# A fifth weight buffer, another place for the first pair of chunks, and later block sums in a one-layer encoder kernel

## The chip, the cores and the metric

The kernel runs on one core of one Trainium2 chip. A core has a matrix engine (TensorE, PE in the rows; PEld are its weight loads), a vector engine (VectorE, DVE), a scalar engine (ScalarE, ACT), GpSimd (POOL) and a sync engine (SyncE, SP), which here only issues DMA transfers. Each engine works through its own queue in order; semaphores tie the queues together. The metric is the device time of one execution in microseconds (us), lower is better.

## The reference

One layer of an encoder on 256 tokens of width 1024, all in float32:

```
x <- x + 1/2 * RMSNorm(SwiGLU(RMSNorm(x)))      first FFN, w_in 1024 x 5632, w_down 2816 x 1024
x <- x + RMSNorm(mix(RMSNorm(x)))               gated recurrence and forgetting attention, merged
x <- x + RMSNorm(CrossAttn(RMSNorm(x), mem))    memory of 256 rows, 4 heads
x <- x + 1/2 * RMSNorm(SwiGLU(RMSNorm(x)))      second FFN

def swiglu(h, w_in, w_down):
    gate, up = jnp.split(h @ w_in, 2, axis=-1)
    return (jax.nn.silu(gate) * up) @ w_down
```

## The kernel before

Every float32 product is made of three matmuls. An operand is split into a rounded part `hi` and the rest `lo`; the product is hi·hi + hi·lo + lo·hi. ScalarE makes `hi` by a cast, VectorE makes `lo` by a subtraction (`load_split`, lines 128 to 138, and `split`, lines 154 to 156). So each weight tile of 128x1024 (512 KB) goes DMA into a `raw` buffer, ScalarE cast, VectorE subtraction, TensorE. There are four `raw` buffers, eight `hi` and eight `lo` buffers, and two `wide` buffers of twice a raw's size. Activations and sums lie in 21 tiles of the pool `data` (`m4`).

The FFN (`ffn`, lines 384 to 695) has 11 chunks of 256 hidden columns. A plain chunk (`act_tok`) takes four weight tiles and 48 matmuls of 512 columns; the down-projection of a chunk (`down`, two further tiles, two token halves) takes 24. Two chunks in a row can be made together as a pair (`quad`, lines 425 to 581) by a Winograd-like scheme: 7 products of 12 matmuls in place of 8, at the price of sums of weight blocks and of activations (`mixed`, lines 288 to 316). `QUADS_1` names the chunks at which pairs begin in the first FFN, here 3, 6 and 9; the second FFN reads sums that were made earlier and stored in DRAM.

In the first FFN the weight sums are made within the pair. For each of two halves q, two tiles come into `raw` (the blocks B11 and B21) and two into one `wide` buffer. VectorE adds: t1 = B11 + first wide block (line 485), t2 = t1 + second wide block (line 465), t4 = t2 - in place with B21 (line 467), and for the third product the two wide blocks (line 498). `rest` makes t2 and t4 together: for q = 0 at once, for q = 1 behind the first down-projection in the code. TensorE then runs: B11 and B21 (24 matmuls, into `b1` and `b3`), the t1 product (12), half of a down-projection (12), the t2 product (12), its other half (12), the product of the wide sums, a whole down-projection (24), the product with the lower wide blocks (`lower`), and the t4 product. `keep` copies a PSUM bank on ScalarE; line 545 adds `b3` to the first of these copies, `p1`. The raw buffers of a pair stay in use until t4 is made, the wide buffers until `lower` is split.

At the head (lines 700 to 725) eight tiles `head` bring x transposed and the first weights. Four of them lie in the four raw buffers, four in the two wide buffers. ScalarE and VectorE split them; then eight ScalarE copies with a gain make `full1`, the unsplit activations that `mixed` reads.

Instructions are put in order by a scheduler that goes by priorities, buffers and dependences; `tc.issue_after(i)` keeps an instruction behind instruction i. So an edit in the code can move instructions at other places too. On SP's queue loads stand in one order, and a load whose buffer is not free holds up those behind it.

Of the kernel before, what the change touches and what calls it, by code (L numbers as in the profile page):

```python
# [9 lines left out]
F32 = mybir.dt.float32  # L10
# [3 lines left out]
ALU = mybir.AluOpType  # L14
AX = mybir.AxisListType

P = 128
D = 1024
T = 256
KB = D // P  # L20
# [28 lines left out]
X_AT = 11  # L49


QUADS_1 = (3, 6, 9)
QUADS_2 = (3, 5, 7, 9)

SUMS_AT = (
# [22 lines left out]
def block_kernel(ctx: ExitStack, tc: tile.TileContext, wts, head_in, gf_in, x_in, mem_in, memT_in, cols, rows, fbias, masks, out):  # L78
    nc = tc.nc
    V, S, G, PE = nc.vector, nc.scalar, nc.gpsimd, nc.tensor  # L80

    cp = ctx.enter_context(tc.tile_pool(name="consts", bufs=1))
    wp = ctx.enter_context(tc.tile_pool(name="weights", bufs=4))
    mp = ctx.enter_context(tc.tile_pool(name="data", bufs=21))
    sp = ctx.enter_context(tc.tile_pool(name="small", bufs=8))
    dp = ctx.enter_context(tc.tile_pool(name="dram", bufs=1, space=bass.MemoryType.DRAM))
    pp = ctx.enter_context(tc.tile_pool(name="psum", bufs=2, space=bass.MemoryType.PSUM))
# [14 lines left out]
    def nm(s):  # L102
        count[0] += 1
        return f"{s}_{count[0]}"
# [22 lines left out]

    def load_split(src, n=512):

        raw = wp.tile([P, D], F32, tag="raw", name=nm("raw"), bufs=4)  # L130
        hi, lo = parts_of()
        r, h, l = raw, hi, lo
        if n < 512:
            r, h, l = (p.rearrange("p (k n) -> p k n", k=2)[:, :, :n] for p in (raw, hi, lo))
        loads.append(nc.sync.dma_start(r, src).ins)
        S.copy(h, r)  # L136
        V.tensor_tensor(out=l, in0=r, in1=h.bitcast(F32), op=ALU.subtract)  # L137
        return hi, lo
# [245 lines left out]
    def ffn(w_in, w_dn, X, full, r2, n_tok, i_row, quads, sums, first_half, second_half=None):  # L384
# [40 lines left out]
        def quad(c, n_down):  # L425
# [12 lines left out]
            if sums:  # L438
                for i in range(4):
                    hi, lo = load_split(wts[_AT[w_in] + 4 * c + i - 4])  # L440
                    B11.append((hi[:, :512], lo[:, :512]))
                    B21.append((hi[:, 512:], lo[:, 512:]))

                def sum_of(k):
                    W = wp.tile([P, 2, D], F32, tag="wide", name=nm("wide"), bufs=2)
                    for q in range(2):
                        with tc.issue_after(loads[-1]):
                            loads.append(nc.sync.dma_start(W[:, q], sums[c][(0, 3, 2, 1)[k], q]).ins)
                    return two(W[:, 0].rearrange("p (i n) -> p i n", i=2)) + two(W[:, 1].rearrange("p (i n) -> p i n", i=2))

                def lower():
                    out = []
                    for q in range(2):
                        u = _AT[w_in] + 4 * c + 2 * q
                        raw = wp.tile([P, D], F32, tag="raw", name=nm("raw"), bufs=4).rearrange("p (i n) -> p i n", i=2)
                        loads.append(nc.sync.dma_start(raw, wts[u : u + 2, :, 512:].rearrange("i p n -> p i n")).ins)
                        out += two(raw)
                    return out

                summed = None  # L460
            else:
                wide, made = [], [[], [], []]

                def rest(W, raws, t1, t2, t4):
                    V.tensor_tensor(out=t2, in0=t1, in1=W[:, :, 1], op=ALU.add)  # L465
                    for i in range(2):
                        V.tensor_tensor(out=t4[:, i], in0=t2[:, i], in1=raws[i][:, 512:], op=ALU.add)  # L467

                for q in range(2):
                    W = wp.tile([P, 2, 2, 512], F32, tag="wide", name=nm("wide"), bufs=2)  # L470
                    raws = []
                    for i in range(2):
                        u = _AT[w_in] + 4 * c + 2 * q + i
                        raw = wp.tile([P, D], F32, tag="raw", name=nm("raw"), bufs=4)
                        loads.append(nc.sync.dma_start(raw, wts[u - 4]).ins)
                        loads.append(nc.sync.dma_start(W[:, i].rearrange("p j n -> p (j n)"), wts[u]).ins)
                        hi, lo = parts_of()
                        split(hi, lo, raw)
                        B11.append((hi[:, :512], lo[:, :512]))
                        B21.append((hi[:, 512:], lo[:, 512:]))  # L480
                        raws.append(raw)
                    wide.append(W)
                    t1, t2, t4 = (m4([P, 2, 512], n="sum") for _ in range(3))
                    for i in range(2):
                        summed = V.tensor_tensor(out=t1[:, i], in0=raws[i][:, :512], in1=W[:, i, 0], op=ALU.add).ins  # L485
                    for k, t in zip((0, 1, 2), (t1, t2, t4)):
# [43 lines left out]
            b1, b2, b3 = mm(), mm(), trp()  # L530
            n = len(log)
# [10 lines left out]
                    flush(n + L_ACT)  # L542
            p1 = keep(b1)
            prods(b2, F(s1h, s1l), T1, True)
            V.tensor_tensor(out=p1, in0=p1, in1=b3, op=ALU.add)
# [15 lines left out]
            n = len(log)  # L561
# [16 lines left out]
            n = len(log)  # L578
# [50 lines left out]
        for c in range(n_tok, NFF):  # L629
# [9 lines left out]
            if c == 2 and first_half:  # L639
                n = len(log)  # L640
# [4 lines left out]
            else:  # L645
                for h in range(2):
                    n = len(log)
# [16 lines left out]
            while done < min(c - 1, NFF - STAG):  # L664
                n = len(log)
# [32 lines left out]


    X1 = Pair()  # L700
    heads = [wp.tile([P, D], F32, tag="raw", name=nm("head"), bufs=4) for kb in range(4)]
    for _ in range(2):
        wide = wp.tile([P, 2, D], F32, tag="wide", name=nm("head"), bufs=2)
        heads += [wide[:, 0], wide[:, 1]]
# [15 lines left out]
        gain_split(X1, kb, heads[kb][:, :T], heads[kb][:, T + 512 + kb : T + 512 + kb + 1], first=kb == 0)  # L720
        lo_last = V.tensor_tensor(out=lo, in0=w, in1=hi.bitcast(F32), op=ALU.subtract).ins
    full1 = [m4([P, 4, T], n="full") for _ in range(2)]
    for kb in range(KB):
        with tc.issue_after(lo_last):
            S.activation(full1[kb // 4][:, kb % 4], heads[kb][:, :T], AF.Copy, scale=heads[kb][:, T + 512 + kb : T + 512 + kb + 1])

# [525 lines left out]
    for h in range(2):  # L1252
# [4 lines left out]
        for i in range(4):  # L1257
            for j in range(2):
                kb = 2 * i + j
# [59 lines left out]
    def second(m):  # L1319
        half(X4, r4, 1, G_F2, m + L_F2)  # L1320
# [87 lines left out]
```

## Time and profile before

| what | us |
| --- | --- |
| runs | 787.92, 788.52, 791.23 (median 788.52) |
| the profiled execution | 787.54 |
| its span in the trace | 785.8 |
| of that, TensorE busy | 772.8 |
| mean granted TensorE clock | 0.999 |
| first FFN, first matmul on real data to the last of its pairs | about 5 to 170 |
| last FFN | about 600 to 786 |

In rows of groups and of the timeline stand the start or the busy time, the engine, the line of the kernel, the operation, and its tiles as output<-inputs; in brackets stands how long the engine was idle before and which instruction ended that. A matmul's shown duration includes the pipeline's drain, so two in a row overlap; the rate is read from start to start. In stretches of time ("a:b") the columns are the length, the busy time and count of each engine, the granted clock, the DMA engines' share and GB/s.

### The profile page before, as it was taken

Reading aid. Unit: us, or ns where it says so; the run is one execution under the profiler, and the core shown is the slowest. Engines: PE = TensorE matmul, PEld = TensorE weight load, DVE = VectorE, ACT = ScalarE, POOL = GpSimd, SP = SyncE. Lnnn points to the kernel's source line nnn. Section 1 sums busy time; section 2 is a strip of 40 time slices with the busy share of each in tenths; the row PEclk is TensorE's granted clock in tenths of the full one; section 3 lists DMA queues with packets and bytes.
Section 4 is the critical chain, followed back from the end, with each engine's and each line's share of the span. In section 5 each row is a group of like instructions: output and inputs, shape, how many; then the busy total and the mean of one; then the engine's idle time right before and its main releaser. Section 6 shows DMA issues by size and latency. Waiting matters only on the chain.

```text
span 785.8 us, 13132 instructions
## 1 busy us (share of the span) xinstructions
PE 772.8 (98%) x4984; PEld 665.8 (85%) x4984; DVE 647.1 (82%) x998; ACT 475.3 (60%) x715; POOL 48.1 (6%) x80
## 2 busy tenths in 40 slices
PE   9999999999999899999999999999999999999996
PEld 7868888877899899998888888999888888888885
DVE  6899898999788788578678887997797988888864
ACT  7757566576654356446685434754655767777752
POOL 0000000000111100200001221012110000000000
PEclk9999999999999999999999999999999999999999
DMA  7848649348688554673389999579966199889931
GB/s 268 299 186 261 225 156 305 119 152 302 252 305 299 184 176 143 216 261 108 133 281 331 375 365 363 200 260 360 361 201 210 57 335 366 323 276 325 348 113 55
DMA packets 57391, 193.61 MB, mean 246 GB/s; under 512 B 6248, under 2 KB 9712, under 8 KB 57328
## 3 DMA queue, kind: packets, MB, share of 16 engines
q1 hardware_dynamic: 48080, 159.60, 58.1%
q0 software_dynamic: 9104, 33.04, 11.8%
q8 instruction: 39, 0.64, 0.3%
q14 instruction: 24, 0.20, 0.1%
q10 hardware_dynamic: 144, 0.13, 0.1%
HBM read 174.92 MB, written 17.83 MB: 245 GB/s over the span
## 4 chain that ended last, share of the span: by engine, by line
PE 87%; DVE 5%; DMA 3%; ACT 2%; issue 1%; SPq 0%; DVEq 0%; ACTq 0%
PE mm L92 59%; PE acc L92 22%; PE tr L92 3%; DMA raw<-in_wts_dram 2%; DVE lo L156 2%; PE tr L324 1%; PE tr L399 1%; DMA head<-in_head_dram 1%; DVE lo L137 1%; ACT hi L136 1%; DVE sum L467 0%; DVE at L420 0%; DVE sum L465 0%; DVE sum L485 0%; DVE act L156 0%
## 5 line engine op out<-in xcount | busy, mean ns | idle before, releaser
L137 DVE TENSOR_TENSOR lo<-raw,hi 128x1024 fp32r<-128x1024 f32 (+1 forms) x220 | 261.1, 1201 | 57.6 <-ACT hi L136 53.9
L136 ACT CAST hi<-raw 128x1024 fp32r<-128x1024 f32 (+1 forms) x220 | 223.9, 1035 | 126.0 <-PE mm L92 65.7
L92 PE MATMUL mm<-hi,lT 128*128 128x512 f32 (+1 forms) x424 | 161.0, 384 | 2.1 <-issue 2.1
L92 PE MATMUL mm<-lo,hT 128*128 128x512 f32 (+1 forms) x424 | 161.9, 385 | 1.1 <-DVE lo L156 1.1
L92 PE MATMUL mm<-hi,hT 128*128 128x512 f32 (+1 forms) x424 | 161.4, 384 | 0.0
L92 PE MATMUL acc<-hi,act 128*128 128x512 f32 x352 | 113.3, 391 | 0.2 <-ACT hi L136 0.2
L92 PE MATMUL mm<-hT,lo 128*128 128x256 f32 x384 | 109.0, 284 | 0.0
L92 PE MATMUL mm<-hT,hi 128*128 128x256 f32 x384 | 109.0, 284 | 0.0
L92 PE MATMUL mm<-lT,hi 128*128 128x256 f32 x384 | 108.9, 284 | 0.0
L92 PEld LDWEIGHTS mm<-hi,hT 128*128 128x128 f32 x424 | 79.6, 188 | 17.4 <-issue 2.3
L92 PEld LDWEIGHTS mm<-lo,hT 128*128 128x128 f32 x424 | 79.5, 188 | 15.5 <-DVE lo L156 1.5
L92 PEld LDWEIGHTS mm<-hi,lT 128*128 128x128 f32 x424 | 79.5, 188 | 14.9 <-DVE lT L286 0.5
L92 PEld LDWEIGHTS acc<-hi,act 128*128 128x128 f32 x352 | 65.8, 188 | 14.4 <-ACT hi L136 0.6
L92 PEld LDWEIGHTS mm<-hT,lo 128*128 128x128 f32 x384 | 73.6, 192 | 0.1
L92 PEld LDWEIGHTS mm<-lT,hi 128*128 128x128 f32 x384 | 73.6, 192 | 0.1
L92 PEld LDWEIGHTS mm<-hT,hi 128*128 128x128 f32 x384 | 73.6, 192 | 0.1
L92 PE MATMUL acc<-lo,act 128*128 128x512 f32 x176 | 69.0, 393 | 0.1
L156 DVE TENSOR_TENSOR lo<-wide,hi 128x1024 fp32r<-128x1024 f32 x44 | 52.3, 1217 | 4.2 <-ACT hi L155 3.8
L155 ACT CAST hi<-wide 128x1024 fp32r<-128x1024 f32 x44 | 45.8, 1052 | 12.6 <-PE mm L92 4.9
L790 POOL DMA_DIRECT2D sums<-wide x32 | 23.6, 737 | 362.8 <-DVE wide L787 245.1
L92 PE MATMUL mm<-lo,sh 128*128 128x512 f32 x112 | 44.0, 392 | 0.2 <-DVE lo L156 0.2
L92 PE MATMUL mm<-hi,sh 128*128 128x512 f32 x112 | 44.0, 393 | 0.0
(248 smaller groups left out, 1160.6 us busy)
## 6 DMA issues: line engine op xcount, KB each, us to landing
raw<-in_wts_dram SPq DMA_DIRECT2D x228, 512.0 KB, 5.2
sums<-wide POOLq DMA_DIRECT2D x32, 512.0 KB, 6.2
wide<-sums SPq DMA_DIRECT2D x32, 512.0 KB, 7.0
wide<-in_wts_dram POOLq DMA_DIRECT2D x28, 512.0 KB, 6.2
wide<-in_wts_dram SPq DMA_DIRECT2D x16, 512.0 KB, 6.8
raw<-in_gf_dram SPq DMA_DIRECT2D x12, 344.0 KB, 5.2
head<-in_head_dram SPq DMA_DIRECT2D x8, 388.0 KB, 6.1
grow<-in_rows_dram SPq DMA_DIRECT2D x4, 512.0 KB, 7.9
```

The costliest lines, as they stand in the source:

```text
L92: log.append(PE.matmul(*args, **kw).ins)
L136: S.copy(h, r)
L137: V.tensor_tensor(out=l, in0=r, in1=h.bitcast(F32), op=ALU.subtract)
L155: S.copy(hi, src)
L156: V.tensor_tensor(out=lo, in0=src, in1=hi.bitcast(F32), op=ALU.subtract)
L324: PE.transpose(ps[:, j * P : (j + 1) * P], src(kb), ident)
L399: PE.transpose(trv[:, j, h * P : (h + 1) * P], ats[c, h][:, j * P : (j + 1) * P], ident)
L790: G.dma_start(sums[u][2 * e : 2 * e + 2, q, :, i * 512 : i * 512 + 512].rearrange("k p n -> p k n"), W[:, e])
```

## The change

There is a fifth raw buffer, and the data pool has 20 tiles in place of 21. The first FFN's pairs begin at chunks 4, 6 and 9, so that chunk 3 is a plain chunk and the pairs at 4 and 6 stand back to back; before, chunk 5 lay between. `rest` is cut into `second` (t2) and `fourth` (t4). For q = 0 both still run at once. For q = 1 `second` stands where `rest` stood, and `fourth` goes to the place where the third product's sums are made; both these and it are kept behind the addition of line 545 by `issue_after(first[0])`, and the two sums of wide blocks now stand ahead of the splits of both. In the head, `full1[0]` is made by one VectorE addition of the split parts; ScalarE keeps its copies for the other four blocks only.

```diff
-QUADS_1 = (3, 6, 9)
+QUADS_1 = (4, 6, 9)
...
-    mp = ctx.enter_context(tc.tile_pool(name="data", bufs=21))
+    mp = ctx.enter_context(tc.tile_pool(name="data", bufs=20))
...
-        raw = wp.tile([P, D], F32, tag="raw", name=nm("raw"), bufs=4)
+        raw = wp.tile([P, D], F32, tag="raw", name=nm("raw"), bufs=5)
...
-                def rest(W, raws, t1, t2, t4):
+                def second():
                     V.tensor_tensor(out=t2, in0=t1, in1=W[:, :, 1], op=ALU.add)
+
+                def fourth():
                     for i in range(2):
                         V.tensor_tensor(out=t4[:, i], in0=t2[:, i], in1=raws[i][:, 512:], op=ALU.add)
...
                     if q == 0:
-                        rest(W, raws, t1, t2, t4)
+                        second()
+                        fourth()
...
-                    out = []
-                    for W in wide:
-                        V.tensor_tensor(out=W[:, :, 0], in0=W[:, :, 0], in1=W[:, :, 1], op=ALU.add)
-                        out += two(W[:, :, 0])
-                    return out
+                    with tc.issue_after(first[0]):
+                        for W in wide:
+                            V.tensor_tensor(out=W[:, :, 0], in0=W[:, :, 0], in1=W[:, :, 1], op=ALU.add)
+                        fourth()
+                    return two(wide[0][:, :, 0]) + two(wide[1][:, :, 0])
...
             T1 = sum_of(0)
+            first = []
...
-            V.tensor_tensor(out=p1, in0=p1, in1=b3, op=ALU.add)
+            first.append(V.tensor_tensor(out=p1, in0=p1, in1=b3, op=ALU.add).ins)
...
             if not sums:
-                rest(W, raws, t1, t2, t4)
+                second()
...
     full1 = [m4([P, 4, T], n="full") for _ in range(2)]
-    for kb in range(KB):
+    V.tensor_tensor(out=full1[0], in0=X1.h[0].bitcast(F32), in1=X1.l[0].bitcast(F32), op=ALU.add)
+    for kb in range(4, KB):
         with tc.issue_after(lo_last):
             S.activation(full1[kb // 4][:, kb % 4], heads[kb][:, :T], AF.Copy, scale=heads[kb][:, T + 512 + kb : T + 512 + kb + 1])
```

Where this moves instructions: first VectorE, in the pair at 6, from the second sums to the splits of the third product's sums. `sum` are t1, t2, t4; `wide` the wide buffers; `keep` is p1. The pair before:

```order
L156 TENSOR_TENSOR lo_1036<-sum_920,hi_1035 128x1024
L156 TENSOR_TENSOR act_766<-tr_982,act_766 128x512
L545 TENSOR_TENSOR keep_989<-keep_989,tr_957 128x512
L465 TENSOR_TENSOR sum_943<-sum_942,wide_927 128x1024
L420 SCALAR_TENSOR_TENSOR at_1006<-keep_989,r_301,sg_1004 128x256
L467 TENSOR_TENSOR sum_944<-sum_943,raw_928 128x512
L467 TENSOR_TENSOR sum_944<-sum_943,raw_935 128x512
L156 TENSOR_TENSOR lo_1040<-sum_943,hi_1039 128x1024
L156 TENSOR_TENSOR lo_1071<-wide_904,hi_1070 128x1024
L498 TENSOR_TENSOR wide_927<-wide_927 128x2x512
L156 TENSOR_TENSOR lo_1076<-wide_927,hi_1075 128x1024
```

The pair at the same place now:

```order
L548 TENSOR_TENSOR keep_983<-keep_983,tr_944 128x512
L137 TENSOR_TENSOR lo_1016<-raw_1014,hi_1015 128x1024
L420 SCALAR_TENSOR_TENSOR at_1000<-keep_983,r_298,sg_998 128x256
L465 TENSOR_TENSOR sum_930<-sum_929,wide_914 128x1024
L156 TENSOR_TENSOR lo_1028<-sum_907,hi_1027 128x1024
L500 TENSOR_TENSOR wide_891<-wide_891 128x2x512
L156 TENSOR_TENSOR lo_1032<-sum_930,hi_1031 128x1024
L500 TENSOR_TENSOR wide_914<-wide_914 128x2x512
L469 TENSOR_TENSOR sum_931<-sum_930,raw_915 128x512
L469 TENSOR_TENSOR sum_931<-sum_930,raw_922 128x512
L156 TENSOR_TENSOR lo_1066<-wide_891,hi_1065 128x1024
L156 TENSOR_TENSOR lo_1070<-wide_914,hi_1069 128x1024
```

The t4 additions (line 467, now 469) for q = 1 have gone behind the split of the second t2, and both sums of wide blocks (line 498, now 500) stand behind the p1 addition; before, the first of them stood between the t1 splits.

Next TensorE, in the same pair, at the t2 product and the down-projection half behind it. `mm` is the product's bank, `acc` the down-projection's, `sh` and `sl` the mixed activations, `act` the activations of an earlier chunk. Before, the twelve matmuls of the product stood together, and the down-projection half followed:

```order
L92 MATMUL mm_955<-hi_1035,sh_341 128x512
L92 MATMUL mm_955<-lo_1036,sh_341 128x512
L92 MATMUL mm_955<-hi_1035,sl_342 128x512
L92 MATMUL mm_955<-hi_1035,sh_341 128x512
L92 MATMUL mm_955<-lo_1036,sh_341 128x512
L92 MATMUL mm_955<-hi_1035,sl_342 128x512
L92 MATMUL mm_955<-hi_1039,sh_341 128x512
L92 MATMUL mm_955<-lo_1040,sh_341 128x512
```

Now:

```order
L92 MATMUL mm_942<-hi_1027,sh_434 128x512
L92 MATMUL acc_444<-hi_1003,act_608 128x512
L92 MATMUL acc_444<-lo_1004,act_608 128x512
L92 MATMUL acc_444<-hi_1003,act_608 128x512
L92 MATMUL acc_445<-hi_1003,act_608 128x512
L92 MATMUL mm_942<-lo_1028,sh_434 128x512
L92 MATMUL mm_942<-hi_1027,sl_435 128x512
L92 MATMUL mm_942<-hi_1027,sh_434 128x512
L92 MATMUL mm_942<-lo_1028,sh_434 128x512
L92 MATMUL mm_942<-hi_1027,sl_435 128x512
L92 MATMUL mm_942<-hi_1031,sh_434 128x512
L92 MATMUL acc_445<-lo_1004,act_608 128x512
```

Four matmuls of the down-projection stand ahead of the first `lo` of the second sums, and four more ahead of the second; the other four follow the product.

Last SP's queue, at the loads of the pair at 6. The loads of lines 475 and 476 (now 477 and 478) are the pair's raw and wide tiles, those of line 135 other weights. Before:

```order
L476 DMA wide_904<-in_wts_dram 128x1024 x2
L476 DMA wide_927<-in_wts_dram 128x1024
L135 DMA raw_866<-in_wts_dram 128x1024
L135 DMA raw_878<-in_wts_dram 128x1024
L475 DMA raw_905<-in_wts_dram 128x1024
L475 DMA raw_912<-in_wts_dram 128x1024
L475 DMA raw_928<-in_wts_dram 128x1024
L475 DMA raw_935<-in_wts_dram 128x1024
L476 DMA wide_927<-in_wts_dram 128x1024
```

Now:

```order
L477 DMA raw_892<-in_wts_dram 128x1024
L477 DMA raw_899<-in_wts_dram 128x1024
L477 DMA raw_915<-in_wts_dram 128x1024
L477 DMA raw_922<-in_wts_dram 128x1024
L135 DMA raw_1002<-in_wts_dram 128x1024
L478 DMA wide_891<-in_wts_dram 128x1024 x2
L478 DMA wide_914<-in_wts_dram 128x1024 x2
L135 DMA raw_1014<-in_wts_dram 128x1024
```

Three of the four wide loads stood ahead of the pair's raw loads; now all four stand behind them and behind a down-projection tile.

More of the change, by code (lines that the diff above doesn't have):

```diff
@@ L454, in lower @@
                         u = _AT[w_in] + 4 * c + 2 * q
-                        raw = wp.tile([P, D], F32, tag="raw", name=nm("raw"), bufs=4).rearrange("p (i n) -> p i n", i=2)
+                        raw = wp.tile([P, D], F32, tag="raw", name=nm("raw"), bufs=5).rearrange("p (i n) -> p i n", i=2)
                         loads.append(nc.sync.dma_start(raw, wts[u : u + 2, :, 512:].rearrange("i p n -> p i n")).ins)
@@ L473, in quad @@
                         u = _AT[w_in] + 4 * c + 2 * q + i
-                        raw = wp.tile([P, D], F32, tag="raw", name=nm("raw"), bufs=4)
+                        raw = wp.tile([P, D], F32, tag="raw", name=nm("raw"), bufs=5)
                         loads.append(nc.sync.dma_start(raw, wts[u - 4]).ins)
@@ L700, in block_kernel @@
     X1 = Pair()
-    heads = [wp.tile([P, D], F32, tag="raw", name=nm("head"), bufs=4) for kb in range(4)]
+    heads = [wp.tile([P, D], F32, tag="raw", name=nm("head"), bufs=5) for kb in range(4)]
     for _ in range(2):
```

## The prediction, made before the changed kernel was run

> **What bounds the kernel now.** I read the page's table of busy time first, then busy time by stretch, then where TensorE's own queue has holes, then what ends each hole.
>
> ```profile
> PE 772.8 (98%) x4984; PEld 665.8 (85%) x4984; DVE 647.1 (82%) x998; ACT 475.3 (60%) x715; POOL 48.1 (6%) x80
> ...
> 46.20:58.50 12.30, 10.67 (x46) 7.41 (x44) 12.30 (x16) 7.09 (x9) 0.00 (x0) 1.00 0.25 89
> 91.40:123.00 31.60, 31.60 (x142) 25.91 (x141) 30.15 (x34) 20.14 (x25) 0.00 (x0) 1.00 0.50 161
> 139.50:173.00 33.50, 33.18 (x149) 26.84 (x149) 32.10 (x37) 22.06 (x28) 0.00 (x0) 1.00 0.39 129
> 268.00:275.00 7.00, 4.92 (x153) 4.79 (x152) 4.62 (x8) 1.11 (x2) 2.27 (x6) 1.00 0.81 301
> 215.00:630.00 415.00, 412.80 (x3360) 372.56 (x3358) 334.96 (x582) 230.01 (x374) 44.76 (x70) 1.00 0.71 248
> 630.00:786.00 156.00, 148.72 (x676) 122.29 (x674) 122.03 (x144) 102.85 (x131) 0.00 (x0) 0.99 0.74 267
> ```
>
> The columns of a stretch are its length, then busy us of TensorE, weight loads, VectorE, ScalarE, GpSimd, then granted clock, DMA share, GB/s. TensorE is the bound, and the change removes no matmul. So only holes can be won. From 215 us on there are 2.2 us of them up to 630 and 7.3 after, most of those behind the last matmul. What is left lies in the first FFN, in two places:
>
> ```profile
> 16.09 0.61 PE L92 MATMUL acc<-lo,hT 128*128 128x512 f32 x2
> 17.27 0.73 PE L92 MATMUL acc<-hi,hT 128*128 128x512 f32 x2 [0.56 <-ACT hi L136]
> 18.59 0.73 PE L92 MATMUL acc<-lo,hT 128*128 128x512 f32 x2
> ...
> 28.68 0.61 PE L92 MATMUL mm<-hi,hT 128*128 128x512 f32 x2
> 29.13 0.62 PE L92 MATMUL mm<-hi,lT 128*128 128x512 f32 x2
> ...
> 50.05 0.39 PE L92 MATMUL mm<-hi,hT 128*128 128x512 f32 x1
> 51.55 0.50 PE L92 MATMUL mm<-lo,hT 128*128 128x512 f32 x1 [1.11 <-DVE lo L156]
> 55.75 1.22 PE L92 MATMUL acc<-hi,act 128*128 128x512 f32 x4 [0.22 <-ACT hi L136]
> 58.49 0.50 PE L92 MATMUL acc<-lo,act 128*128 128x512 f32 x1
> ...
> 102.04 0.60 PE L399 MATMUL tr<-ident,at 128*128 128x128 f32 x4
> 102.40 0.48 PE L92 MATMUL tr<-lo,hT 128*128 128x512 f32 x1
> ```
>
> Two matmuls take 0.45 from start to start (28.68 to 29.13), so one is 0.2265; four transposes take 0.36 (102.04 to 102.40). From 16.09 to 18.59 six matmuls should take 1.36 and took 2.50: **1.1 lost** at the head. From 50.05 to 58.49 the timeline has 23 matmuls and four transposes, 5.6 at that rate, and took 8.4: **2.9 lost** in the first pair (chunks 3 and 4). The chain of waits shows why:
>
> ```profile
> 33.76 7.07 DMA raw<-in_wts_dram
> 57.30 1.15 DVE lo L137
> 58.49 4.17 PE acc L92 x17
> ```
>
> Up to 58 us the path runs through weight loads and VectorE, afterwards through TensorE. In the stretch from 46.2 to 58.5 the loads run at 89 GB/s: all four raw buffers are held for the pair's sums, and the down-projection weights that TensorE takes at 55.75 and 58.49 come late. So 4.0 us is about all that this change can gain there, 0.5% of the time. A measurement of this kernel tells some 0.5%, 3.9 us, from no change.
>
> **The change part by part.** The fifth raw buffer and the head's copies:
>
> ```profile
> 0.75 4.26 SPq L706 DMA_DIRECT2D head<-in_head_dram  x8
> 11.66 3.44 SPq L135 DMA_DIRECT2D raw<-in_wts_dram  x4
> GB/s 0 91 279 392 334 381 381 403 414 144 8 153 342 295 218 299 371 397 422 404 386 408 379 273 269 76 73 259 197 240 361 288 262 335 397 430 415 415 422 397
> ...
> 13.78 2.50 ACT L725 ACTIVATE full<-head 128x256 f32<-128x256 f32 x6
> 16.18 1.03 ACT L136 CAST hi<-raw 128x1024 fp32r<-128x1024 f32 x1
> ```
>
> The GB/s row covers 0 to 45 us, 1.125 us a cell. The head tiles hold all four raw buffers, so the first weights are issued at 11.66, and the DMA engines nearly stop from 10 to 13.5 us. A fifth buffer lets one load follow the heads at 5 us; the others come free with the head splits instead of with ScalarE's copies. ScalarE makes its first weight cast at 16.18, right behind six copies; the change drops four copies of 0.41 (2.50 over six), 1.6 us, so that cast is ready near 15.6, before TensorE wants it at 16.5. VectorE gets one 128x1024 addition (1.14, below) between the head's splits, where it has idle time and TensorE is some 1 us behind it; that covers nearly all of it. Without cover it costs 1.1 and the head gains nothing. I take 1.1 won and 0.2 paid: **-0.9** (bounds -1.1 and 0).
>
> Pairs at 4, 6, 9. I follow VectorE's lead: from the end of the first split of a pair's weights to the first matmul that reads it.
>
> ```profile
> 32.52 1.21 DVE L137 TENSOR_TENSOR lo<-raw,hi 128x1024 fp32r<-128x1024 f32 x1
> 86.04 2.48 DVE L156 TENSOR_TENSOR lo<-raw,hi 128x1024 fp32r<-128x1024 f32 x2 [0.90 <-ACT hi L155]
> 104.90 0.67 DVE L545 TENSOR_TENSOR keep<-keep,tr 128x512 f32<-128x512 f32 x1
> 106.63 0.48 DVE L420 SCALAR_TENSOR_TENSOR at<-keep,r,sg 128x256 f32<-128x256 f32 x1
> 107.03 1.28 DVE L467 TENSOR_TENSOR sum<-sum,raw 128x512 f32<-128x512 f32 x2
> 108.23 1.21 DVE L156 TENSOR_TENSOR lo<-sum,hi 128x1024 fp32r<-128x1024 f32 x1
> 109.37 1.21 DVE L156 TENSOR_TENSOR lo<-wide,hi 128x1024 fp32r<-128x1024 f32 x1
> 112.95 1.23 DVE L156 TENSOR_TENSOR lo<-wide,hi 128x1024 fp32r<-128x1024 f32 x1 [1.24 <-ACT hi L155]
> 122.20 4.62 DVE L137 TENSOR_TENSOR lo<-raw,hi 128x1024 fp32r<-128x1024 f32 x4
> ...
> 97.28 0.39 PE L92 MATMUL mm<-lo,hT 128*128 128x512 f32 x1
> 110.00 0.39 PE L92 MATMUL mm<-lo,sh 128*128 128x512 f32 x1
> 127.88 0.40 PE L92 MATMUL mm<-lo,hT 128*128 128x512 f32 x1
> ```
>
> From start to start an operation on 128x1024 takes 1.14 (108.23 to 109.37), on 128x512 0.60 (half of 107.03 to 108.23), on 128x256 0.40 (106.63 to 107.03). In the pair at 6 the first split ends near 87.3 and is read at 97.28: a lead of 10.0. The second half of the second sums ends at 109.4 and is read at 110.0: 0.6. At the pair's end the next chunk's first split ends near 123.4, read at 127.88: 4.5. So a pair eats VectorE's lead and a plain chunk restores it; the first pair began with too little.
>
> The pair at 4: VectorE's order after the fourth split of chunk 2 (ends 33.7) has, up to the pair's first split: 11 of 1.14, 8 mix additions of about 0.37, 3 of 0.60, 2 of 0.40: 18.1, so 51.8. TensorE, from chunk 2's start at 28.68, has 144 matmuls and 12 transposes, 33.7, less 1.1 won at the head: 61.3. Lead 9.5, near the 10.0 seen. The largest fall inside a pair in the new order comes at the third sums: 14 of 1.14, 12 of 0.60, 3 of 0.40, 24.3 on VectorE, against 72 matmuls and 8 transposes, 17.0, on TensorE: 7.3. The 9.5 cover it. The 2.9 go: **-2.8**, with 0.1 left.
>
> The pair at 6, now directly behind it: From the one pair's first split to the other's VectorE has 33.2 (22 of 1.14, 11 of 0.60, 4 of 0.40), TensorE 30.6 (132 matmuls, 8 transposes): the lead falls to 6.9. By the row at 122.20 it would be 4.5. The fall of 7.3 then leaves TensorE waiting 0.4 or 2.8. TensorE's new order helps at the second sums (down-projection matmuls now stand between their halves), which is why the bottleneck moves to the third. I take **+1.2**, nearer the sum, because the idle 1.24 of the row at 112.95 was the wait for a cast right behind a sum of wide blocks, and that sum now stands earlier.
>
> The third and fourth products' sums behind the first product's addition: the same additions, later: the third sums' two of 1.14 and the fourth's two of 0.60. In the pair at 6 of before, 2.3 us of them stood ahead of what TensorE read next. In the pair at 9 nothing in front of it has moved, and its holes of 0.3 in 33.5 (above) can shrink: **-0.2** (0 to -0.3). They now wait for that addition, which waits for the pair's first 24 matmuls and ScalarE's copy; behind it on VectorE stand a down-projection split and the second sums, for which TensorE waits. By the sums above VectorE gets there 6.9 us of TensorE time into the first pair, just when it is ready, and 1 us after that in the second: a few tenths at most. Raw buffers are held longer for it; the fifth pays for that.
>
> One data tile less: TensorE's order from the mix stage to the second FFN is unchanged; the second FFN has loads issued earlier and no hole to fill: 0, bounds +-0.5.
>
> Sum: -0.9 -2.8 +1.2 -0.2 = **-2.7**. The profiled execution took 787.54 (span 785.8, 1.7 around it), so 784.8 by its own time. The median of the runs shown, 788.52, lies 1.0 higher; between the two I put **785.5**.
>
> **The rivals.**
> (1) The second pair gives it back: its hole is 2.8 and more, because the lead at its start is the 4.5 of the row rather than 6.9. For it: that row was measured. Against: that pair's VectorE also idled 1.24. Net -1 to +0.5: 788.
> (2) All holes close: the lead of 9.5 is there and the second pair loses nothing: -4.1, 784.0.
> (3) Slower: the second pair's wide loads come late. Only two wide buffers exist; the pair at 6 gets them when the pair at 4 has split its lowest blocks, and its wide loads now stand behind five raw loads on SP.
>
> ```profile
> wide<-in_wts_dram SPq DMA_DIRECT2D x16, 512.0 KB, 6.8
> wide<-in_wts_dram SPq DMA_DIRECT2D x4, 512.0 KB, 9.0
> ```
>
> From the release to the first addition that needs such a tile VectorE has 6.7 us of work (5 of 1.14, one of 0.60, one of 0.40); the load takes 6.8 over the kernel and, by the row of the first 45 us, 9.0. That is a wait of 0.1 to 2.3, which comes straight off the lead. Past a landing time of about 12 us the wait is 5, the hole 6 to 8, and the kernel slower by 2 to 4: 791.5. Against: only half as many bytes are asked for there as before 45 us (161 against some 300 GB/s). The Trainium skill ("TensorE: Matmul & The Clock Gate", section "Part 1: The HAM clock gate") says that about 3.4 us of idle halves TensorE's clock until it has been busy as long again; by that a hole of 6 would cost some 2 to 3 more, an estimate from that page. The longest hole here, 2.1 us in the stretch 268 to 275, shows the clock at 1.00; no longer one is in this trace.
> (4) The fifth buffer does not do it at the head, since ScalarE, not the load, releases 17.27: then the dropped copies carry it alone, and 0.5 of the 0.9 is missing; inside the forecast's range.
>
> **How the numbers follow.** Forecast (783.9 to 787.0) 0.46; rival 1 0.23; rival 2 0.14; rival 3 0.17. Against 788.52 faster by over 0.5% means under 784.6: rival 2 and a sixth of the forecast, 0.22. Slower means over 792.5: somewhat over half of rival 3 and a little of what I have not seen, 0.14. The rest, 0.64, is within. Range: 783.0, all holes closed at the lower base, to 791.0, rival 1 at the upper base with a waiting wide load.
>
> **What would show it.** The holes at 16 to 19 and in the first pair are gone; SP issues the first raw load at 5 us; the lead at the two pairs' first splits reads 9 to 10 and 6 to 7; TensorE's first long wait in the first FFN is at the third sums of the second pair, released by VectorE's split or by an addition that waits for a wide load. I am wrong if the first pair still waits (loads, not order, set its lead), if the hole in the second pair is over 3 us, or if anything behind 215 us moves by more than 1 us.

## The result, and the profile after

The changed kernel takes **784.12 us** (median of 7 runs, 783.06 to 785.23); the kernel before, on the same chip, 788.16 (785.70 to 791.23). The ratio is **0.9944, 95% interval 0.9923 to 0.9965**: 4.4 us saved, at least 2.8 and at most 6.1. The forecast was 785.5. The profiled executions' spans are 785.8 and 782.5.

Busy time, and the same stretches that the prediction shows of before (length, then TensorE, weight loads, VectorE, ScalarE, GpSimd, clock, DMA share, GB/s); first the page, then the view by stretch:

```profile
PE 771.1 (99%) x4984; PEld 666.3 (85%) x4984; DVE 648.1 (83%) x999; ACT 473.0 (60%) x711; POOL 49.2 (6%) x80
```

```profile
46.20:58.50 12.30, 12.30 (x56) 10.18 (x55) 11.34 (x13) 5.46 (x8) 0.00 (x0) 1.00 0.73 257
91.40:123.00 31.60, 30.95 (x139) 24.60 (x137) 31.55 (x37) 22.07 (x28) 0.00 (x0) 1.00 0.56 193
139.50:173.00 33.50, 33.50 (x154) 27.63 (x153) 33.22 (x39) 23.74 (x30) 0.00 (x0) 1.00 0.50 171
215.00:630.00 415.00, 412.54 (x3342) 371.27 (x3342) 334.84 (x578) 226.45 (x371) 45.86 (x70) 1.00 0.70 245
```

TensorE had 10.67 of 12.30 us in the first of these stretches and has all of it now; in the second it had all and now lacks 0.65; behind 215 us almost nothing moved. The timeline of the changed kernel on SP, TensorE and VectorE shows it at each step of the prediction:

```profile
5.11 4.16 SPq L135 DMA_DIRECT2D raw<-in_wts_dram  x4
...
27.68 0.62 PE L92 MATMUL mm<-hi,hT 128*128 128x512 f32 x2
...
50.85 1.22 DVE L156 TENSOR_TENSOR lo<-raw,hi 128x1024 fp32r<-128x1024 f32 x1
...
62.01 0.39 PE L92 MATMUL mm<-lo,hT 128*128 128x512 f32 x1
...
85.34 2.35 DVE L156 TENSOR_TENSOR lo<-raw,hi 128x1024 fp32r<-128x1024 f32 x2
...
92.42 0.39 PE L92 MATMUL mm<-lo,hT 128*128 128x512 f32 x1
...
109.50 0.39 PE L92 MATMUL acc<-hi,act 128*128 128x512 f32 x1
110.39 0.49 PE L92 MATMUL mm<-hi,sh 128*128 128x512 f32 x1 [0.49 <-ACT keep L529]
111.04 0.50 PE L92 MATMUL mm<-lo,sh 128*128 128x512 f32 x1 [0.16 <-DVE lo L156]
111.38 0.40 PE L92 MATMUL mm<-hi,sl 128*128 128x512 f32 x1
...
124.81 0.39 PE L92 MATMUL mm<-lo,hT 128*128 128x512 f32 x1
...
194.43 1.03 PE L324 MATMUL tr<-ident,xs 128*128 128x128 f32 x8
```

Chunk 2's first matmul starts at 27.68 instead of 28.68. The first pair's first split ends at 52.1 (50.85 and 1.22) and is read at 62.01: a lead of 9.9. The second pair's ends at 86.6 and is read at 92.42: 5.9. From 109.50 to 111.38 three matmuls, 0.7 at full rate, took 1.9: 1.2 lost, at the third sums of the second pair. The matmul that stood at 127.88 now stands at 124.81. The last row, the second group of transposes of xs, is the mark that I use below for the end of the first FFN; in the kernel before it reads:

```profile
198.32 1.03 PE L324 MATMUL tr<-ident,xs 128*128 128x128 f32 x8
```

So the first FFN ends 3.9 us earlier, and 0.6 of it is gone by the end of the span.

### The profile page after: what moved, and what is told of

Its sections match the earlier page's. It is cut to its first block, busy times and chain, and to the rows that moved or that the text cites. A ratio compares the mean times of both kernels' runs of the same rounds, so it can differ in the third digit from the quotient of the medians.

```text
span 782.5 us, 13109 instructions
## 1 busy us (share of the span) xinstructions
PE 771.1 (99%) x4984; PEld 666.3 (85%) x4984; DVE 648.1 (83%) x999; ACT 473.0 (60%) x711; POOL 49.2 (6%) x80
## 4 chain that ended last, share of the span: by engine, by line
PE 89%; DVE 7%; DMA 1%; issue 1%; ACT 1%; SPq 0%; DVEq 0%; ACTq 0%
PE mm L92 59%; PE acc L92 24%; PE tr L92 3%; DVE lo L156 2%; DVE lo L137 1%; PE tr L324 1%; PE tr L399 1%; DMA raw<-in_wts_dram 1%; DMA head<-in_head_dram 1%; DVE sum L469 1%; DVE wide L500 1%; DVE sum L487 0%; DVE sum L465 0%; ACT hi L155 0%; PE tr L1082 0%
```

## The experiments

The change has four parts, and each was tried alone on the kernel before and taken out of the changed kernel; then three other combinations, and the changed kernel again. Each kernel was timed 12 times, beside 35 runs of the kernel before. "Copies" stands for the split of the head's copies. Chunk 2 and the mark (the end of the first FFN) are read from TensorE's timeline of each one's profiled execution. The last column says how far the time of that execution lies from the kernel's own median; where it is large, at pairs alone, without buffer, and copies and pairs, the mark is likely later than a usual execution of that kernel would show.

| kernel | raw buffers | pairs | copies | sums | ratio to before | interval | chunk 2 at | mark at | traced, from median |
|---|---|---|---|---|---|---|---|---|---|
| before | 4 | 3, 6, 9 | 8 | old | 1 | | 28.68 | 198.32 | -0.6 |
| buffer alone | 5 | 3, 6, 9 | 8 | old | 0.9956 | 0.9938 to 0.9973 | 28.35 | 194.99 | +1.1 |
| pairs alone | 4 | 4, 6, 9 | 8 | old | 1.0031 | 1.0010 to 1.0052 | 28.66 | 201.98 | +3.6 |
| copies alone | 4 | 3, 6, 9 | 4 | old | 0.9972 | 0.9956 to 0.9988 | 27.88 | 196.99 | +0.1 |
| sums alone | 4 | 3, 6, 9 | 8 | new | 1.0002 | 0.9986 to 1.0019 | 28.30 | 197.77 | +0.1 |
| without buffer | 4 | 4, 6, 9 | 4 | new | 0.9981 | 0.9960 to 1.0002 | 27.82 | 198.03 | +2.4 |
| pairs back | 5 | 3, 6, 9 | 4 | new | 0.9966 | 0.9946 to 0.9985 | 27.08 | 193.83 | -0.5 |
| copies back | 5 | 4, 6, 9 | 8 | new | 0.9965 | 0.9951 to 0.9979 | 29.17 | 195.13 | -0.2 |
| sums back | 5 | 4, 6, 9 | 4 | old | 0.9963 | 0.9949 to 0.9976 | 27.77 | 194.95 | 0.0 |
| copies and pairs | 4 | 4, 6, 9 | 4 | old | 0.9972 | 0.9952 to 0.9992 | 27.27 | 199.39 | +3.9 |
| buffer and copies | 5 | 3, 6, 9 | 4 | old | 0.9963 | 0.9944 to 0.9983 | 27.47 | 195.10 | 0.0 |
| pairs at 4, 7, 9 | 5 | 4, 7, 9 | 4 | new | 1.0032 | 1.0010 to 1.0054 | 27.16 | 200.15 | +0.5 |
| changed, again | 5 | 4, 6, 9 | 4 | new | 0.9946 | 0.9925 to 0.9967 | 27.32 | 194.26 | +0.4 |

### The buffer alone

```diff
-    mp = ctx.enter_context(tc.tile_pool(name="data", bufs=21))
+    mp = ctx.enter_context(tc.tile_pool(name="data", bufs=20))
-        raw = wp.tile([P, D], F32, tag="raw", name=nm("raw"), bufs=4)
+        raw = wp.tile([P, D], F32, tag="raw", name=nm("raw"), bufs=5)
```

(and the same number at the other raw and head tiles)

> The kernel before with the fifth raw buffer alone (and one data tile less). Theory A (the terms add: head about -1.0, first pair about -2.9 by its place, second pair about +0.9): the first raw load is issued near 5 us instead of 11.66, but the weights' first cast still stands behind eight copies on ScalarE, so at most half of the head's hole closes; the pair at 3 still waits some 2.5 to 2.9. About -0.5 us, 0.9994 of before. Theory B (the buffer carries the gain, since the first pair's holes come from held raw buffers): the first pair's holes shrink to under 1, and the time falls by 2.5 to 3.5, ratio about 0.996.

Theory B. 0.0044 of 788 is **3.5 us**, with the first pair at its old place. The waits of the pair at 3 go back to late loads. ScalarE's casts in the kernel before:

```profile
38.28 1.05 ACT L155 CAST hi<-raw 128x1024 fp32r<-128x1024 f32 x1 [1.53 <-DMA raw<-in_wts_dram]
40.86 1.05 ACT L155 CAST hi<-raw 128x1024 fp32r<-128x1024 f32 x1 [1.52 <-DMA raw<-in_wts_dram]
```

VectorE, in order behind them, in the kernel before:

```profile
36.30 1.23 DVE L137 TENSOR_TENSOR lo<-raw,hi 128x1024 fp32r<-128x1024 f32 x1 [1.04 <-ACT hi L136]
...
39.37 1.23 DVE L156 TENSOR_TENSOR lo<-raw,hi 128x1024 fp32r<-128x1024 f32 x1 [1.25 <-ACT hi L155]
...
41.94 1.23 DVE L156 TENSOR_TENSOR lo<-raw,hi 128x1024 fp32r<-128x1024 f32 x1 [1.35 <-ACT hi L155]
```

and with the fifth buffer alone:

```profile
35.47 1.22 DVE L137 TENSOR_TENSOR lo<-raw,hi 128x1024 fp32r<-128x1024 f32 x1
...
37.20 1.22 DVE L156 TENSOR_TENSOR lo<-raw,hi 128x1024 fp32r<-128x1024 f32 x1
...
39.28 1.23 DVE L156 TENSOR_TENSOR lo<-raw,hi 128x1024 fp32r<-128x1024 f32 x1 [0.86 <-ACT hi L155]
```

The three splits waited 3.6 us and now wait 0.9. TensorE reads the pair's first split at 46.20 and at 45.87 (the second matmul of the pair in each timeline), so the lead there goes from 5.6 to 7.4, and TensorE is busy for 37.64 of the 38 us from 28 to 66, before for 36.37.

### The pairs' places alone

```diff
-QUADS_1 = (3, 6, 9)
+QUADS_1 = (4, 6, 9)
```

> The kernel before with the pairs at 4, 6, 9 alone, four raw buffers. Theory A: the head's hole of 1.1 stays, the first pair's 2.9 close to 0.3 or less, and the second pair pays 1 to 2: -1 to -2 us, ratio 0.9975 to 0.9987. Theory B (the buffer is what closes the first pair): the first pair still waits 2 or more wherever it stands, and the second loses on top of it: +0.5 to +2, ratio 1.001 to 1.0025.

Theory B by time, and more than it said: **2.4 us slower** (0.8 to 4.1). In the trace the mark is 3.7 late, but the holes do not lie where theory B had them. VectorE does not start the first split of the pair at 4 at 50.85 but here:

```profile
55.03 1.22 DVE L156 TENSOR_TENSOR lo<-raw,hi 128x1024 fp32r<-128x1024 f32 x1
```

TensorE reads it at 64.79, a lead of 8.5, and does not wait for it. VectorE's waits for casts of weights between 10 and 65 us:

```profile
DVE lo L137 <- ACT hi L136: 6.7, 6, 2.7
```

That is 6.7 us in six waits. Three of them, 5.1 us, lie before 24 us, at the first weights. There the kernel before makes the eight mix additions (14.71 to 20.84), which now stand from 43.05 on. The other three, 1.6 us, lie at the splits from 36 to 41 us. So the split from which the prediction counts, the fourth of chunk 2, ends at 34.4 (33.7 before, 30.3 in the changed kernel), and from there to the end of the pair's first split VectorE takes 21.9 us here and 21.8 in the changed kernel. What makes the pair late is the late weights at the head: with the copies dropped as well, the same split ends at 52.5 (copies and pairs, below). TensorE pays for it ahead of the pair:

```profile
47.48 0.44 PE L399 MATMUL tr<-ident,at 128*128 128x128 f32 x2 [1.20 <-DVE at L420]
```

and behind 100 us, where the kernel before has no hole up to 170, in holes of up to 0.77. The wait moved; it did not go.

### The head's copies alone

```diff
-    for kb in range(KB):
+    V.tensor_tensor(out=full1[0], in0=X1.h[0].bitcast(F32), in1=X1.l[0].bitcast(F32), op=ALU.add)
+    for kb in range(4, KB):
```

> The kernel before with only the head's first four ScalarE copies replaced by one VectorE addition. Theory A with the head's gain shared: the first raw cast comes up to 1.6 us earlier on ScalarE but the loads are still issued near 11 us; -0.4 to -0.6 of the 1.1, and nothing else moves. Rival (the dropped copies alone carry the head): -1.0, hole at 16 to 19 us gone. Rival (the load is what was late): 0. All within 0.9985 to 1.0005; the trace decides, by the start of chunk 2's first matmul (28.68 before, 27.7 in the changed kernel).

The first rival, that the copies alone carry the head: chunk 2 starts at 27.88. The loads are not "still issued near 11 us", as I had expected; SP in this kernel, with four raw buffers:

```profile
5.49 4.94 SPq L135 DMA_DIRECT2D raw<-in_wts_dram  x4
```

The head tiles leave the raw buffers when their last reader is done, and the last readers were ScalarE's copies (`full`). SP's waits for them in the kernel before:

```profile
SPq L135 <- ACT full L725: 7.7, 3, 5.9
```

Over all kernels: eight copies give a start between 28.30 and 29.17, five buffers or four; four copies between 27.08 and 27.88, five buffers or four. The total, 2.2 us less (0.9 to 3.5), is more than the head and, by its middle, more than any of the three theories had: the loads behind it come earlier as well.

### The sums alone

```diff
-                    if q == 0:
-                        rest(W, raws, t1, t2, t4)
+                    if q == 0:
+                        second()
+                        fourth()
                 def sum_of(k):
...
+                    with tc.issue_after(first[0]):
+                        for W in wide:
+                            V.tensor_tensor(out=W[:, :, 0], in0=W[:, :, 0], in1=W[:, :, 1], op=ALU.add)
+                        fourth()
```

> The kernel before with only the third and fourth products' sums moved behind the first product's addition, pairs at 3, 6, 9, four raw buffers. Theory A: the pair at 3 keeps its holes (2.5 to 3), since what is late there is VectorE's lead at the pair's start; the pairs at 6 and 9 gain 0.2 to 0.4 together; raw buffers are held longer, which may cost as much. -0.4 to +0.5 us. Rival (the order of the sums carries the gain): the holes of the pair at 3 fall to under 1, -2 us or more, ratio 0.9975 or less.

Theory A by time: no difference (0.2 us, -1.1 to +1.5). The holes are not quite as it has them: in the trace the pair at 3 has three of 0.31, 0.56 and 0.16 us where the kernel before has 1.11, 0.22 and 0.22, and one of 0.93 opens at 91.18.

### One part taken out of the changed kernel

Without the buffer:

```diff
-    mp = ctx.enter_context(tc.tile_pool(name="data", bufs=20))
+    mp = ctx.enter_context(tc.tile_pool(name="data", bufs=21))
-        raw = wp.tile([P, D], F32, tag="raw", name=nm("raw"), bufs=5)
+        raw = wp.tile([P, D], F32, tag="raw", name=nm("raw"), bufs=4)
```

> The changed kernel with four raw buffers and the 21st data tile again, all else kept. Theory A: half of the head's 1.0 comes back and the longer-held raw buffers make the pairs' loads late by some tenths: +0.5 to +1.5 against the changed kernel, -2 to -3 against before, ratio 0.996 to 0.9975. Theory B (the buffer carries it): the pair at 4 waits 2 or more again, the time is back at the kernel before's, ratio 0.9995 or more.

Between the two theories in time, 1.5 us under before (0.2 over to 3.2 under), and neither in place. The pair at 4 waits for nothing here (TensorE is busy for all of 28 to 66 us). The largest holes come at the pair at 9, in TensorE's timeline of this kernel:

```profile
166.22 0.49 PE L92 MATMUL mm<-hi,hT 128*128 128x512 f32 x1 [0.35 <-ACT keep L529]
...
167.41 0.50 PE L92 MATMUL mm<-hi,sh 128*128 128x512 f32 x1 [0.70 <-DVE keep L562]
...
169.75 0.44 PE L410 MATMUL tr<-ident,at 128*128 128x128 f32 x2 [0.46 <-DVE at L420]
```

Pairs back at 3, 6, 9:

```diff
-QUADS_1 = (4, 6, 9)
+QUADS_1 = (3, 6, 9)
```

> The changed kernel with its pairs back at 3, 6, 9. Theory A: the pair at 3 waits 2.5 to 2.9 again, the pair at 6 waits nothing (it has a plain chunk ahead of it): +1.6 to +2.0 against the changed kernel, -1.3 to -1.7 against before, ratio 0.998. Theory B (buffer or sums carry the first pair): the pair at 3 waits under 1, and the time is that of the changed kernel or up to 0.9 below, ratio 0.993 to 0.996.

In the trace theory B: the mark at 193.83 is the earliest of all, and 100 to 130 us are busy throughout. The hole is now in the pair at 3, at the same sums and with the same releasers as the changed kernel's in the pair at 6:

```profile
62.08 0.49 PE L92 MATMUL mm<-hi,sh 128*128 128x512 f32 x1 [0.69 <-ACT keep L529]
62.73 0.50 PE L92 MATMUL mm<-lo,sh 128*128 128x512 f32 x1 [0.16 <-DVE lo L156]
```

With five buffers the pair's place moves a hole of about 1 us from one pair to another. The times (2.7 us under before, against 4.4 and 4.3 for the changed kernel) overlap in their intervals and do not tell the two apart.

The copies back:

```diff
-    V.tensor_tensor(out=full1[0], in0=X1.h[0].bitcast(F32), in1=X1.l[0].bitcast(F32), op=ALU.add)
-    for kb in range(4, KB):
+    for kb in range(KB):
```

> The changed kernel with all eight copies at the head on ScalarE again. Theory A with the head shared: 0.5 of the 1.0 comes back, +0.5 against the changed kernel. Rival (the dropped copies alone carry the head): +1.0, chunk 2's first matmul back at 28.7. Rival (the buffer alone): 0, chunk 2's first matmul near 27.7.

The rival with the copies: chunk 2 back at 29.17, though SP issues its first weights at 4.52. The mark is 0.7 later than the changed kernel's; the time, 2.8 us under before, is not told apart from the changed kernel's.

The old order of the sums:

```diff
-                    if q == 0:
-                        second()
-                        fourth()
+                    if q == 0:
+                        rest(W, raws, t1, t2, t4)
...
-                    with tc.issue_after(first[0]):
```

> The changed kernel with the third and fourth products' sums in their old place. Theory A: the bottleneck of the pair at 6 goes back from the third sums to the second half of the second sums, where 2.3 us of VectorE's work stand ahead of what TensorE reads next; the lead at that pair's first split stays near 5.9, so its holes grow from 1.1 to 2 to 3.4: +1 to +2.3 against the changed kernel, ratio against before 0.9965 to 0.999. Rival (the order of the sums is worth only the 0.2 of the prediction): +0.2 to +0.4.

The mark moves by 0.5, near the rival: with five buffers the order of the sums is worth little. The time, 2.9 us under before, is not told apart from the changed kernel's.

### Two parts together, and another place

```diff
-QUADS_1 = (3, 6, 9)
+QUADS_1 = (4, 6, 9)
-    for kb in range(KB):
+    V.tensor_tensor(out=full1[0], in0=X1.h[0].bitcast(F32), in1=X1.l[0].bitcast(F32), op=ALU.add)
+    for kb in range(4, KB):
```

> The kernel before with the dropped head copies and the pairs at 4, 6, 9; four raw buffers, sums in their old place. Theory C (what the first pair lacks is weights that landed earlier: the dropped copies free the raw buffers at 5 us as a fifth buffer would, and both the head and the pair at 4 then wait for nothing; the later pairs at four buffers wait for loads): lost near 0 between 28 and 63 us, second pair pays 1 to 1.5, 130 to 187 us loses about as much as before (1.5 to 2): the first FFN ends 2 to 3 us earlier than before, ratio 0.9965 to 0.998. Rival (the fifth buffer is needed for the pair at 4): 1.5 or more lost between 28 and 63 us, ratio 0.9995 or more. If 130 to 187 us loses 3 or more, as in the run without the buffer, the moved sums are not what costs it there.

By time theory C: 2.2 us under before (0.6 to 3.8). The trace is of the longest of the twelve executions, so its mark, 1.1 us later than before, is likely later than usual. In it 28 to 63 us lose nothing, as theory C has it, but the pair at 4 waits later on. VectorE and TensorE of this kernel:

```profile
51.26 1.23 DVE L156 TENSOR_TENSOR lo<-raw,hi 128x1024 fp32r<-128x1024 f32 x1
...
61.60 0.39 PE L92 MATMUL mm<-lo,hT 128*128 128x512 f32 x1
...
75.06 1.22 DVE L156 TENSOR_TENSOR lo<-sum,hi 128x1024 fp32r<-128x1024 f32 x1
...
76.33 0.50 PE L92 MATMUL mm<-lo,sh 128*128 128x512 f32 x1 [1.83 <-DVE lo L156]
```

The lead at the pair's first split is 9.1 and at the second half of the second sums zero (75.06 and 1.22 against 76.33). In this execution, in the old order and with four buffers, 9.1 did not cover the pair; whether shorter executions have this hole is not shown. From 130 to 190 us TensorE is idle for 1.02 here and for 1.52 in the run without the buffer, but not at the same place. Here nearly all of it is one hole ahead of the pair at 9, at a down-projection that waits for ScalarE:

```profile
140.59 0.50 PE L92 MATMUL acc<-hi,act 128*128 128x512 f32 x1 [0.92 <-ACT act L155]
```

So of these two kernels only the one with the moved sums has holes in the pair at 9. But the sums alone, with the pairs at 3, 6 and 9, lose 0.02 in that stretch, and these are one trace each: what costs the run without the buffer its 1.52 is not shown.

```diff
-        raw = wp.tile([P, D], F32, tag="raw", name=nm("raw"), bufs=4)
+        raw = wp.tile([P, D], F32, tag="raw", name=nm("raw"), bufs=5)
-    for kb in range(KB):
+    V.tensor_tensor(out=full1[0], in0=X1.h[0].bitcast(F32), in1=X1.l[0].bitcast(F32), op=ALU.add)
+    for kb in range(4, KB):
```

> The kernel before with the fifth raw buffer and the dropped head copies, nothing else: pairs at 3, 6, 9, old order of the sums. Theory C (early weights are the gain, the place of the pair is not): head's hole gone, the pair at 3 loses about 1 to 1.5, the pair at 6 nothing: as good as the changed kernel or up to 0.7 better, ratio 0.993 to 0.996. Theory A (the pair's place carries 2.9): 2 us worse than the changed kernel, ratio 0.997 or more.

Theory C: 2.9 us under before without touching the pairs or the sums, the mark 0.8 behind that of the changed kernel run beside it. By time its interval holds both theories' values.

```diff
-QUADS_1 = (4, 6, 9)
+QUADS_1 = (4, 7, 9)
```

> The changed kernel with its pairs at 4, 7, 9: a plain chunk between the first two pairs, none between the last two. Theory (a pair eats VectorE's lead and a plain chunk restores it): the hole of 1.1 in the second pair goes, and comes back in the third, which is now directly behind; the net is 0 to -0.7 against the changed kernel, ratio 0.993 to 0.996. Rival (the hole belongs to the second pair's own order, not to the lead): it stays at 1.1 wherever that pair stands.

The theory holds at both pairs and misses the total. The second pair waits for nothing (by stretch):

```profile
100.00:130.00 30.00, 30.00 (x138) 24.82 (x137) 29.75 (x33) 20.34 (x25) 0.00 (x0) 1.00 0.44 141
```

and 0.7 come back in the third, at its third sums (TensorE, three matmuls in 1.41):

```profile
156.70 0.39 PE L92 MATMUL acc<-hi,act 128*128 128x512 f32 x1
157.08 0.50 PE L92 MATMUL mm<-hi,sh 128*128 128x512 f32 x1
157.77 0.50 PE L92 MATMUL mm<-lo,sh 128*128 128x512 f32 x1 [0.18 <-DVE lo L156]
158.11 0.40 PE L92 MATMUL mm<-hi,sl 128*128 128x512 f32 x1
```

But then, at the end of the FFN, on ScalarE, VectorE and TensorE:

```profile
185.47 1.04 ACT L136 CAST hi<-raw 128x1024 fp32r<-128x1024 f32 x1 [2.53 <-DMA raw<-in_wts_dram]
...
186.54 1.22 DVE L137 TENSOR_TENSOR lo<-raw,hi 128x1024 fp32r<-128x1024 f32 x1 [2.08 <-ACT hi L136]
187.69 1.41 DVE L351 SCALAR_TENSOR_TENSOR xs<-post,y,xs 128x512 f32<-128x512 f32 x2
...
188.53 1.94 PE L324 MATMUL tr<-ident,xs 128*128 128x128 f32 x8 [5.33 <-issue]
```

xs, which TensorE needs, stands on VectorE behind a split whose weights landed late. In that stretch the DMA engines are full (393 GB/s, in the last section), after moving only 141 GB/s between 100 and 130 us. The kernel is **2.5 us slower than before** (0.8 to 4.3), and by the medians 6.6 slower than the changed one beside it.

The changed kernel again:

> The changed kernel again, on the same chip and beside the same runs of before as the other three, so that versions that differ by some tenths of a us can be set beside it: 0.9944 within its interval of 0.9923 to 0.9965.

4.3 us under before: the same.

No version beats the changed kernel by time; the pairs back at 3 with the rest kept ends the first FFN 0.4 to 0.6 earlier in one trace each, which the times don't bear out.

## Why the prediction came out as it did

| term | predicted | in the trace |
|---|---|---|
| head | -0.9 | -1.0 (28.68 to 27.68) |
| pair at 4 | -2.8 | -2.9 (no hole left) |
| pair at 6 | +1.2 | +1.2 (109.50 to 111.38) |
| sums, pair at 9 | -0.2 | -0.8 |
| one data tile less | 0 | 0 (412.80 and 412.54 busy) |

The -0.8 is the difference between the two marks (198.32 less 194.43, 3.9) and the gain at chunk 8 (127.88 less 124.81, 3.1). To chunk 8 the terms give -2.7, so 0.4 of small holes has no term. From the marks to the span's end 0.6 is lost again; the changed kernel's second execution differs from its first by 1.2 over that same stretch (span less mark), so that part says nothing. That stretch takes 587.9 to 590.1 us in the eight traces with 20 data tiles and 587.5 to 590.1 in the six with 21: no cost of the tile shows. The median lies 1.4 under the forecast.

**The sizes were right and the cause of the largest was not.** The step that failed is "the first pair began with too little", with the 2.8 credited to the pair's place. The sum behind it, 18.1 of VectorE's work from 33.7 to 51.8, has no wait for a load in it. That 52.1 came out is luck, two errors that cancel: because the other parts brought the loads forward, VectorE starts that stretch at 30.3, 3.4 earlier, and it then takes 21.8 for it, 3.7 more, of which 2.9 are two waits for casts of activations. By place alone the split ends at 56.3 and the kernel loses 2.4. The two rows that should have warned stood in the prediction: the chain's 7.07 of a raw load at 33.76, and the 89 GB/s. I named the held raw buffers there and then costed the fifth one at the head only. What the place does is what I said of the lead (9.9, 9.1 and 8.5 at a pair at 4, 5.6 and 7.4 at a pair at 3), but with late loads the 8.5 is paid for by holes elsewhere, and with five buffers 7.4 is nearly enough.

**Early weights decide, and the fifth buffer brings the most.** Apart from the kernel with pairs at 4, 7, 9, the mark stands between 193.83 and 195.13 in all kernels with five buffers, and between 196.99 and 201.98 in all with four; three of the latter traces are of executions 2.4 to 3.9 us over the median. The ratios are 0.9944 to 0.9966 with five and 0.9972 to 1.0031 with four. Alone the buffer is worth 3.5 us; taken out of the four it costs 2.9 by the two ratios, whose intervals just overlap. The dropped copies alone are worth 2.2, and by time that is not told apart from the buffer alone.

**Head.** Right in size, by the mechanism of rival 4: the copies carry it. "A fifth buffer lets one load follow the heads at 5 us" is true and wins little there: alone it lets the first load go at 4.64, and SP then waits 7.4 us for ScalarE's copies, before 7.7.

**The pair at 6.** Right in size and place, but in part by luck. The lead was 5.9, between the 6.9 of the sum and the 4.5 of the row, and the wait is at the third sums. Of the 1.2 the sum knows only VectorE's part: the matmul at 111.04 is 0.4 late and waits for its split. The one at 110.39 is 0.7 late and waits for ScalarE's copy of a bank (`keep`), which stands behind a cast that had itself waited for TensorE; no term had that. ScalarE and VectorE:

```profile
108.80 1.05 ACT L155 CAST hi<-wide 128x1024 fp32r<-128x1024 f32 x1 [1.30 <-PE mm L92]
109.75 0.58 ACT L529 COPY keep<-mm 128x512 f32<-128x512 f32 x1
...
108.56 1.28 DVE L469 TENSOR_TENSOR sum<-sum,raw 128x512 f32<-128x512 f32 x2
109.77 2.35 DVE L156 TENSOR_TENSOR lo<-wide,hi 128x1024 fp32r<-128x1024 f32 x2
```

The moved fourth sums (108.56) stand just ahead of the split. Rival 3 is out: VectorE's view of waits is empty for 63 to 115 us, so no wide load held it up. Rival 2's time, 784.0, is almost the measured one, but its condition is not met.

**The moved sums.** -0.2 was too little for that stretch, and the sums are not shown to be its cause: alone they change the time by nothing, the old order in the changed kernel moves the mark by 0.5, and with pairs at 3, 6, 9 (buffer and copies, against pairs back) by 1.3, 0.4 of it at the head. That they help a little once there are five buffers is likely; how the 0.8 is shared between them and the buffer stays open.

## What to carry to other kernels

When one engine's lead over another is the quantity that counts, follow the lead back to the transfer that set it before moving the work that uses it up: here earlier loads restored the lead in place, and moving the work without them lost time. A buffer is held by its last reader, so a copy on an engine that is not the bottleneck can delay a transfer that the others need. Parts of one edit that close the same hole are not worth the sum of what each is worth alone: the buffer 3.5 and the copies 2.2, together 2.9 (1.3 to 4.4).

## What the runs showed of the hardware

After a hole of about 2 us TensorE's clock fell to half in some executions and not in others. Each of the fourteen traces has a hole of 1.1 to 2.6 us between 265 and 277 us, behind the first FFN:

| clock behind it | holes, us |
|---|---|
| 0.50 for a while, eight traces | 2.08 (pairs at 4, 7, 9), 2.18, 2.28, 2.39 (changed, again), 2.39, 2.46, 2.48, 2.64 |
| 1.00 throughout, six traces | 1.13, 1.81, 2.00, 2.08 (before), 2.13 (changed), 2.57 (pairs alone) |

So the length alone does not decide it. From the mark to the end of the span the eight take 589.1 to 590.1 us; of the six, five take 587.5 to 588.5 and the pairs alone 590.1. The changed kernel's two executions, 1.2 apart there, are one of each kind. The one such hole that the prediction had seen, 2.1 us with the clock at 1.00 behind it, was one of two outcomes.

The copies-and-pairs kernel shows it in the first FFN too, behind its hole of 1.83 us, by stretch (the clock is the third figure from the end):

```profile
76.40:78.00 1.60, 1.60 (x5) 1.27 (x6) 1.60 (x2) 1.60 (x3) 0.00 (x0) 0.61 0.87 330
78.00:80.20 2.20, 2.20 (x7) 1.72 (x6) 2.20 (x3) 2.11 (x3) 0.00 (x0) 0.51 0.40 160
```

Ten matmuls from 76.33 to 80.31 took 0.40 each instead of 0.2265: 1.7 us, nearly as much as the hole itself. Behind the 5.33 of the kernel with pairs at 4, 7, 9:

```profile
183.00:188.50 5.50, 0.20 (x1) 0.00 (x0) 3.38 (x6) 1.04 (x1) 0.00 (x0) 0.82 1.00 393
188.50:190.50 2.00, 1.97 (x9) 1.99 (x10) 0.94 (x2) 1.56 (x5) 0.00 (x0) 0.50 1.03 422
```

There the clock fell within the hole, about 3.3 us from its start (1.00 up to 186 us, 0.76 in the next one, 0.50 from 187 on), and it stayed at half until 193.5, where the matmuls' spacing is 0.23 again. The Trainium skill ("TensorE: Matmul & The Clock Gate", section "Part 1: The HAM clock gate") has the clock halve after an idle window of about 3.4 us and come back after a busy one as long, with windows that run freely. The hole of 5.33 agrees in the fall; the way back took 5.0 us. Holes of 1.8 to 2.6, shorter than such a window, were followed by half clock as well, and there the measurement decides.
